# Moving the projections' evacuations behind the transposes in slots 57 to 84 of a hybrid attention trunk

## The chip, the cores and the metric

The kernel runs on one core of a Trainium2 chip. The metric is the device time in microseconds; the median of three runs of the kernel before is 633.63 us (633.28 to 633.99). PE is the matrix engine, ACT, DVE and POOL are the three elementwise engines, SP issues nearly all DMAs.

## The reference

Two layers of an encoder over 512 frames of width 1024. In each, one input projection feeds two groups of eight heads of width 64: group A is stick-breaking attention, group B softmax attention over the top 128 keys that an indexer picks, with a relative bias. Both groups are gated, concatenated and projected out; a residual and a layer norm follow.

```python
proj = jnp.einsum('bsd,dn->bsn', x, w_in)
qA, kA, vA, gA, qB, kB, vB, gB, qI, kI, wI = jnp.split(proj, SPLIT_POINTS, axis=-1)
oA = stick_breaking_attention(heads(qA, HEADS_A), heads(kA, HEADS_A), heads(vA, HEADS_A))
oB = dsa_sparse_attention(heads(qB, HEADS_B), heads(kB, HEADS_B), heads(vB, HEADS_B),
                          qI.reshape(b, s_len, IDX_HEADS, IDX_DIM), kI, wI, rel_bias, topk)
mix = jnp.concatenate([oA * jax.nn.silu(gA), oB * jax.nn.silu(gB)], axis=-1)
y = jnp.einsum('bsm,md->bsd', mix, w_out)
return layer_norm(ALPHA * x + y, ln_g, ln_b)
```

## The kernel before, in words

All matrix products are done in pairs of a high and a low half: a number is rounded to the fast format (high half, a copy on ACT), and what the rounding lost is kept as a low half (a subtraction on DVE or POOL). A projection is three matmuls for each of eight slices of the width: high by high, low by high, high by low.

The order on PE, ACT, DVE and POOL is the order in which the Python code issues (the pools run under a manual schedule). Each of these engines takes its instructions one after the other. The order on SP is made by the framework.

A layer is a loop over slots (variable `s`). Slots 0 to 23 are the indexer. From slot 24 on each slot is one block of 128 queries of one head: group A in slots 24 to 55, group B in slots 56 to 87. Head h of group B has slots 56 + 4h to 59 + 4h; its blocks `qb` 0 to 3 see 128, 256, 384 and 512 keys, so the width of an instruction tells its block. What one block of group B (class `Soft`) does is spread over several slots:

- in the slot before: POOL adds bias and mask into `p` (L821), unless that sum was stored before by DVE (L1048)
- in its slot: PE computes `z` (L573, L578); DVE adds the bias, and takes the row minimum `mn` (L830, with a second small instruction that reads `mn` out); ACT computes the exponential and its sums (L835, function `stage1b`)
- two slots later: PE transposes `p` into the PSUM tile `tr` (L585), ACT copies it out as the high half of `AT` (L593), and DVE subtracts for the low half (L596, `evacuate_lo`). For group A these are L795 and L798. There are two `tr` banks and two `z` banks
- three slots later, for the last block of a head: PE multiplies with the values (L769, `start_values` and `rest_of_values`), ACT and DVE combine the halves (L655, L657, `mix`), and POOL multiplies into `M` (L658)

Between these PE runs the projections of the units to come: `fill(...)` steps through them by a table of due times. When an accumulator is done, its evacuation is put in the list `later`, and `flush()` issues what is in the list. An evacuation of k is two ACT copies (L428, L429), two DVE subtractions (L430, L431) and two DMAs that copy halves to the other partitions (L185); of q two copies (L420, L421) and two subtractions (L422, L423); of v one of each (L413, L414); of the output projection one DVE instruction (L859). Accumulators have three PSUM banks (`pj`). The weights come by DMA; `prep_ahead` at the end of a slot splits the next one by ACT (L231) and POOL (L234).

Inside a slot the code issues: `stage0` (z), `stage2`, `stage1` (row minimum), `prepare`, `flush()`, a fill, `transpose` and `evacuate` for the older block, `stage1b` (exponential), `evacuate_lo`, the top-k, a fill, the rest.

Of the kernel before, what the change touches and what calls it, by code (L numbers as in the profile page):

```python
# [44 lines left out]
IDX_SLOTS = 24  # L45
# [24 lines left out]
SUM_SLOTS = 3  # L70
HALF_SLOTS = 5
STAGED = (46, 48)
B_PINS = (59.2, 62.5, 67, 71, 79)


# [3 lines left out]
def fills():  # L79
# [8 lines left out]
    units += [(u, both) for u in (("B", 1, "k"), ("B", 1, "q"), ("B", 1, "v"))]  # L88
    return [(u, cs, by) for (u, cs), by in zip(units, HEAD_PINS + A_PINS + B_PINS, strict=True)]

# [27 lines left out]
def tile_hybrid(ctx: ExitStack, tc: tile.TileContext, xt, x, w_in, w_ki, w_out, ln_g, ln_b, rel_bias, onehot, out, depth=DEPTH):  # L118
# [161 lines left out]
    def flush():  # L280
        while later:
            later.pop(0)()
# [330 lines left out]
    def layer(l):  # L613
# [70 lines left out]
        def split_staged(half):  # L684
            if not half:
                QKV[PAIR[1]] = vp.tile([P, NTB, 4 * P], F32R, tag="v", name="vt")
            t = slice(2 * half, 2 * half + 2)
            vv = QKV[PAIR[1]].rearrange("p t (h r) -> p t h r", r=P)[:, t]
            src = XN[:, t, W256:S].rearrange("p t (h d) -> p t h d", d=HD)
            A.activation(vv[:, :, :, :HD], src, AF.Copy)  # L690
            for i in range(2):
                G.tensor_tensor(vv[:, i, :, HD:], src[:, i], vv[:, i, :, :HD], ALU.subtract)
# [225 lines left out]
        def topk_rounds(upto):  # L918
            while rounds and 48 - len(rounds) < upto:
                qb = rounds.pop(0)  # L920
                m8 = sm.tile([P, 8], F32, tag=f"m8{qb}", name="m8", bufs=2)
                V.max(m8, scores[qb])  # L922
                V.match_replace(scores[qb], m8, scores[qb], TAKEN)  # L923
                if not rounds:
                    for b in range(1, NTB):
                        V.tensor_scalar(mask[b], scores[b], -2.0e38, MASKED, ALU.is_gt, ALU.mult)
# [40 lines left out]
        for s in range(SLOTS + 3):  # L967
# [30 lines left out]
                tasks[s].stage1()  # L998
            if isinstance(at(s + 1), Soft):
                tasks[s + 1].prepare()  # L1000
            flush()
            if not sticks[0]:
                fill(now + FRAC[0])
            for old in olds:
# [7 lines left out]
                tasks[s].stage1b()  # L1012
            for old in olds:
                old.evacuate_lo(old.head.at)
            if s >= IDX_SLOTS:
                topk_rounds(PAUSE + RATE * (s - IDX_SLOTS))
            fill(now + FRAC[1])
# [24 lines left out]
            for h in STORED:  # L1042
                if s == AHEAD[h]:
                    by_number[h].load()
                for qb, (by, tb, col) in STORED[h].items():
                    if s == by:
                        n = P * (qb + 1)
                        V.tensor_tensor(XN[:, tb, col : col + n], by_number[h].g[:, :n][:, ::-1], mask[qb], ALU.add)  # L1048
            if s in STAGED:
                split_staged(STAGED.index(s))  # L1050
            if l == 0 and s in (10, 14):
# [121 lines left out]
    for l in range(depth):  # L1173
        layer(l)
# [49 lines left out]
```

## Time and profile before

| what | value |
|---|---|
| median of 3 runs | 633.63 us |
| the profiled execution's own time | 634.15 us |
| its span | 632.3 us |
| granted clock of PE, mean | 0.998 |
| busy: PE, DVE, ACT, POOL | 620.8, 488.3, 345.2, 364.4 us |

The span runs from the first to the last instruction; 1.85 us of the execution lie around it. Busy time on PE says that matmuls were under way. Times in the timeline are microseconds from the start of the span; line numbers are those of the kernel before. Slots 57 to 84 of the first layer lie at about 196 to 270 us, those of the second layer 310.24 us later. Consecutive equal instructions stand in one row (x2, x4). A bracket at the end of a row is how long the engine stood idle before it, and what ended that.

### The profile page before, as it was taken

What the parts mean: (1) busy time and instruction counts of PE and PEld (TensorE: products, weight loads), DVE (VectorE), ACT (ScalarE), POOL (GpSimd) and SP (SyncE); (2) the same over time, 40 slices, a digit from 0 to 9 for tenths busy, and PEclk for the clock granted to TensorE, in tenths of its full rate; (3) what the DMA queues carried; (4) which work ended last, traced back from release to release, by engine and by line L of the source; (5) the groups of instructions that cost most, each with busy time, mean ns of one, the idle gap of its engine ahead of it and who ended that gap; (6) DMA issues with size and microseconds to landing.
All of it is one profiled execution on the core that took longest, in us unless ns stands there. A gap on an engine that the chain in (4) does not pass through costs nothing.

```text
span 632.3 us, 9889 instructions
## 1 busy us (share of the span) xinstructions
PE 620.8 (98%) x3309; PEld 532.3 (84%) x3309; DVE 488.3 (77%) x1050; ACT 345.2 (55%) x682; POOL 364.4 (58%) x388
## 2 busy tenths in 40 slices
PE   8999999999999999999999999999999999999995
PEld 7988888888887889888899888888888878898884
DVE  2778999899966875668845789998999567756676
ACT  4776544455357566883135855534644566678700
POOL 5553454618856676798134554525585587778721
PEclk9999999999999999999999999999999999999999
DMA  7624332141253475353313243313313444634402
GB/s 222 215 94 121 112 112 91 68 134 67 90 160 98 130 193 168 116 197 119 131 70 133 100 135 100 105 63 133 101 67 114 138 118 136 175 127 141 170 34 100
DMA packets 35688, 77.40 MB, mean 122 GB/s; under 512 B 6642, under 2 KB 15856, under 8 KB 35638
## 3 DMA queue, kind: packets, MB, share of 16 engines
q1 hardware_dynamic: 35350, 76.51, 38.2%
q8 instruction: 26, 0.43, 0.3%
q10 hardware_dynamic: 288, 0.26, 0.1%
q14 instruction: 24, 0.20, 0.1%
HBM read 61.84 MB, written 4.44 MB: 105 GB/s over the span
## 4 chain that ended last, share of the span: by engine, by line
PE 93%; DMA 2%; POOL 1%; ACT 1%; DVE 1%; SPq 1%; issue 0%; DVEq 0%; ACTq 0%; POOLq 0%
PE pj L292 15%; PE pj L294 15%; PE pj L293 15%; PE pjo L877 14%; PE o L769 6%; PE tr L585 5%; PE z L578 4%; PE z L573 4%; PE pjv L363 2%; PE pjv L361 2%; PE pjv L362 2%; PE pjv L329 2%; PE pjv L331 2%; PE pjv L330 2%; PE pjv L483 1%; DMA M<-in_w_ki_dram 1%
## 5 line engine op out<-in xcount | busy, mean ns | idle before, releaser
L234 POOL TENSOR_TENSOR wlo<-raw,whi 128x256 fp32r<-128x256 f32 (+1 forms) x254 | 228.6, 930 | 166.2 <-ACT whi L231 165.6
L292 PE MATMUL pj<-XH,whi 128*128 128x512 f32 (+1 forms) x432 | 172.1, 398 | 0.0
L294 PE MATMUL pj<-XH,wlo 128*128 128x512 f32 (+1 forms) x432 | 166.4, 385 | 0.0
L293 PE MATMUL pj<-XL,whi 128*128 128x512 f32 (+1 forms) x432 | 166.0, 384 | 0.0
L294 PEld LDWEIGHTS pj<-XH,wlo 128*128 128x128 f32 x432 | 81.1, 188 | 16.1
L292 PEld LDWEIGHTS pj<-XH,whi 128*128 128x128 f32 x432 | 81.2, 188 | 12.8
L293 PEld LDWEIGHTS pj<-XL,whi 128*128 128x128 f32 x432 | 81.4, 188 | 12.2
L785 ACT ACTIVATE om<-z 128x128 f32<-128x128 f32 (+1 forms) x64 | 28.0, 438 | 115.8 <-PE z L578 68.9
L231 ACT ACTIVATE whi<-raw 128x1024 fp32r<-128x1024 f32 x78 | 82.0, 1056 | 2.5 <-DMA raw<-in_w_in_dram 2.0
L790 DVE TENSOR_TENSOR_SCAN om<-om,future 128x128 f32<-128x128 f32 (+1 forms) x64 | 65.8, 1028 | 0.1
L922 DVE MAX8 m<-scores 128x8 f32<-128x256 f32 (+2 forms) x96 | 52.8, 550 | 0.2
L923 DVE MATCH_REPLACE8 scores<-m,scores 128x256 f32<-128x256 f32 (+2 forms) x96 | 52.1, 542 | 0.0
L658 POOL TENSOR_TENSOR M<-M,mixt 64x512 f32<-64x512 f32 x22 | 31.4, 1425 | 35.6 <-DVE mixt L657 27.7
L769 PE MATMUL o<-AT,vt 128*128 128x512 f32 (+7 forms) x256 | 48.5, 315 | 0.0
L835 ACT ACTIVATE p<-p,mn 128x128 f32<-128x128 f32 (+1 forms) x64 | 35.8, 560 | 22.0 <-DVE mn L830 21.7
L877 PE MATMUL pjo<-whi,XH 128*128 128x512 f32 (+1 forms) x118 | 41.2, 387 | 0.0
L877 PE MATMUL pjo<-wlo,XH 128*128 128x512 f32 (+1 forms) x118 | 41.0, 384 | 0.0
L578 PE MATMUL z<-k,q 128*128 128x128 f32 (+3 forms) x128 | 40.9, 320 | 0.0
L596 DVE TENSOR_TENSOR AT<-tr,AT 128x128 fp32r<-128x128 f32 (+1 forms) x64 | 31.2, 488 | 11.2 <-ACT AT L593 10.3
L877 PE MATMUL pjo<-whi,XL 128*128 128x512 f32 (+1 forms) x118 | 39.5, 381 | 0.0
L573 PE MATMUL z<-k,q 128*128 128x128 f32 (+3 forms) x128 | 39.2, 306 | 0.0
L769 PEld LDWEIGHTS o<-AT,vt 128*128 128x128 f32 (+1 forms) x256 | 32.9, 162 | 4.7 <-DVE AT L596 1.0
(172 smaller groups left out, 1271.8 us busy)
## 6 DMA issues: line engine op xcount, KB each, us to landing
raw<-in_w_in_dram SPq DMA_DIRECT2D x58, 512.0 KB
k<-k SPq DMA_DIRECT2D x32, 256.0 KB
raw<-in_w_out_dram SPq DMA_DIRECT2D x14, 512.0 KB
gbias<-f_dram SPq DMA_DIRECT2D x18, 256.0 KB
raw<-in_w_in_dram SPq DMA_DIRECT2D x16, 256.0 KB
XN<-in_x_dram SPq DMA_DIRECT2D x8, 256.0 KB
y_dram<-XN SPq DMA_DIRECT2D x4, 512.0 KB
XN<-y_dram SPq DMA_DIRECT2D x8, 256.0 KB
```

Of the source, the lines that this page charges most:

```text
L231: A.activation(hi, src, AF.Copy)
L234: low = lambda lo=lo[:, c], src=src[:, c], hi=hi[:, c]: lo_engine.tensor_tensor(lo, src, hi, ALU.subtract)
L292: T.matmul(o, w[0], XH[:, tb:, kc, :], start=first, stop=False)
L293: T.matmul(o, w[0], XL[:, tb:, kc, :], start=False, stop=False)
L294: T.matmul(o, w[1], XH[:, tb:, kc, :], start=False, stop=last)
L573: T.matmul(self.z[:, :nn], a, b, start=True, stop=False)
L578: T.matmul(self.z[:, :nn], c, d, start=False, stop=True)
L769: T.matmul(self.o[:m, sb * P :], vt[:, sb, self.hh * P : self.hh * P + m], at_block(self.at[j], sb, sb, NTB - sb), start=(sb, j) == (0, 0) ...
L790: V.tensor_tensor_scan(rev, rev, future[:, S - n :][:, ::-1], 1.0, ALU.mult, ALU.max)
L877: T.matmul(acc[:, cols], mixed[:, tb, m, :], w[:, cols], start=n == 0, stop=n == len(steps) - 1)
L922: V.max(m8, scores[qb])
L923: V.match_replace(scores[qb], m8, scores[qb], TAKEN)
```

## The change

In slots 57 to 84 of each layer, `flush()` is called behind `evacuate_lo`, in place of in front of the transposes. In the other slots nothing changes.

```diff
+FLUSH_LATE = range(IDX_SLOTS + 33, IDX_SLOTS + 61)
...
             if isinstance(at(s + 1), Soft):
                 tasks[s + 1].prepare()
-            flush()
+            if s not in FLUSH_LATE:
+                flush()
             if not sticks[0]:
                 fill(now + FRAC[0])
             for old in olds:
                 old.transpose()
                 old.evacuate(old.head.at)
...
             if isinstance(at(s), Soft):
                 tasks[s].stage1b()
             for old in olds:
                 old.evacuate_lo(old.head.at)
+            if s in FLUSH_LATE:
+                flush()
             if s >= IDX_SLOTS:
                 topk_rounds(PAUSE + RATE * (s - IDX_SLOTS))
```

The order on PE and POOL is the same in both programs. On ACT and DVE ten evacuations a layer move: k, q, k, k, q and q in slots 58, 62, 64, 66, 68 and 70; three of v in slots 72, 74 and 76; and one of the output projection in slot 84 (on DVE alone). In the rows of the changed program the line numbers are one to four higher (L836 is L835 of before, L429 is L428, L799 is L798).

ACT in slot 58 of the first layer, before; k is the projection's evacuation, AT the transposes' high half, p,sums the exponential:

```order
L835 ACTIVATE p,sums<-p,mn 128x256
L428 ACTIVATE k<-pj 64x512
L429 ACTIVATE k<-pj 64x512
L795 ACTIVATE AT_107<-tr 128x4x128
L593 ACTIVATE AT_105<-tr 128x128
L835 ACTIVATE p,sums<-p,mn 128x384
L231 ACTIVATE whi_2209<-raw_2047 128x1024
```

and now:

```order
L836 ACTIVATE p,sums<-p,mn 128x256
L796 ACTIVATE AT_107<-tr 128x4x128
L594 ACTIVATE AT_105<-tr 128x128
L836 ACTIVATE p,sums<-p,mn 128x384
L429 ACTIVATE k<-pj 64x512
L430 ACTIVATE k<-pj 64x512
L232 ACTIVATE whi_2209<-raw_2047 128x1024
```

The two copies of k moved past both high halves and past the exponential of the same slot; the weight's split stays behind them.

DVE in the same slot, before; ISA is the row minimum L830, its 128x1 row the reading of mn:

```order
L830 ISA p,mn<-z,p 128x384
L830 ISA mn 128x1
L430 TENSOR_TENSOR k<-pj,k 64x512
L431 TENSOR_TENSOR k<-pj,k 64x512
L798 SCALAR_TENSOR_TENSOR AT_108<-tr,AT_107 128x4x128
L596 TENSOR_TENSOR AT_106<-tr,AT_105 128x128
L830 ISA p,mn<-z,p 128x512
```

and now:

```order
L831 ISA p,mn<-z,p 128x384
L831 ISA mn 128x1
L799 SCALAR_TENSOR_TENSOR AT_108<-tr,AT_107 128x4x128
L597 TENSOR_TENSOR AT_106<-tr,AT_105 128x128
L431 TENSOR_TENSOR k<-pj,k 64x512
L432 TENSOR_TENSOR k<-pj,k 64x512
L831 ISA p,mn<-z,p 128x512
```

The two subtractions for k moved past both low halves, and still stand ahead of the next slot's row minimum.

ACT in slots 67 and 68, before; q is the projection's evacuation:

```order
L835 ACTIVATE p,sums<-p,mn 128x512
L420 ACTIVATE q<-pj 64x512
L421 ACTIVATE q<-pj 64x512
L593 ACTIVATE AT_105<-tr 128x3x128
L835 ACTIVATE p,sums<-p,mn 128x128
L231 ACTIVATE whi_2577<-raw_2392 128x1024
```

and now:

```order
L836 ACTIVATE p,sums<-p,mn 128x512
L594 ACTIVATE AT_105<-tr 128x3x128
L836 ACTIVATE p,sums<-p,mn 128x128
L421 ACTIVATE q<-pj 64x512
L422 ACTIVATE q<-pj 64x512
L232 ACTIVATE whi_2577<-raw_2392 128x1024
```

The q copies moved from in front of slot 68's high half to between its exponential and the weight's split.

## The prediction, as it stood before the result

> **What bounds the kernel now.** I read the page first, then windows of 10 us, then the waits, and last the timeline of the slots concerned.
>
> ```profile
> span 632.3 us, 9889 instructions
> PE 620.8 (98%) x3309; PEld 532.3 (84%) x3309; DVE 488.3 (77%) x1050; ACT 345.2 (55%) x682; POOL 364.4 (58%) x388
> ```
>
> PE sets the end: it is idle for only 632.3 - 620.8 = 11.5 us of the span. PE's own work and order are not touched by the change, so the new time is the old one, less the PE gaps that go, plus those that come. In slots 57 to 84 of the two layers the windows with a gap are these (columns: busy time of PE, PEld, DVE, ACT, POOL):
>
> ```profile
> 200.00:210.00 10.00, 9.08 (x53) 7.53 (x52) 7.48 (x17) 5.82 (x13) 8.14 (x9) 1.00 0.58 163
> 260.00:270.00 10.00, 9.99 (x55) 8.04 (x53) 6.67 (x23) 8.43 (x20) 8.36 (x6) 1.00 0.52 167
> 570.00:580.00 10.00, 9.68 (x53) 7.85 (x52) 6.15 (x23) 8.33 (x21) 7.98 (x6) 1.00 0.54 177
> ```
>
> 0.92 us is missing at 200 to 210 (slot 58), almost nothing in the rest of that layer, and 0.32 us at 574 in the second. The waits name the first gap and show who waits for whom among the helpers (us in total, times, longest):
>
> ```profile
> PE tr L585 <- DVE AT L798: 1.8, 2, 0.9
> ACT p L835 <- DVE mn L830: 21.7, 25, 2.1
> DVE k L430 <- ACT k L429: 17.5, 14, 3.9
> ```
>
> Twice, once a layer, transposes wait 0.92 us for DVE to empty a `tr` bank. The second row matters as much: ACT's exponential L835 often stands waiting for DVE's row minimum. Whatever is put behind L835 waits with it.
>
> **The change part by part.** First the gain, in slot 58 (columns: start, length, engine, line):
>
> ```profile
> 200.04 0.59 ACT L428 ACTIVATE k<-pj 64x512 fp32r<-64x512 f32 x1
> 201.23 0.56 DVE L830 CUSTOM_DVE_ANT_0 p<-z,p 128x384 f32<-128x384 f32 x1 [1.48 <-POOL p L821]
> 201.71 0.68 DVE L430 TENSOR_TENSOR k<-pj,k 64x512 fp32r<-64x512 f32 x1
> 201.92 0.62 ACT L835 ACTIVATE p<-p,mn 128x384 f32<-128x384 f32 x1
> 202.52 1.05 ACT L231 ACTIVATE whi<-raw 128x1024 fp32r<-128x1024 f32 x1
> 203.15 0.69 DVE L798 SCALAR_TENSOR_TENSOR AT<-tr,AT 128x512 fp32r<-128x512 f32 x1
> 203.89 0.44 PE L585 MATMUL tr<-ident,p 128*128 128x128 f32 x2 [0.92 <-DVE AT L798]
> 203.95 0.68 DVE L830 CUSTOM_DVE_ANT_0 p<-z,p 128x512 f32<-128x512 f32 x1
> ```
>
> L430 and L431 take 203.15 - 201.71 = 1.44 us ahead of L798. With them behind, L798 starts about 201.8, ends about 202.5, and PE, ready at 203.89 - 0.92 = 202.97, no longer waits: **-0.92 us a layer**.
>
> The price: ACT did the two k copies from 200.04, before mn was there. Now they stand behind L835, which cannot start before mn (201.8). L835 takes 202.52 - 201.92 = 0.60 until the next start, so L428 starts at 202.5 and L429 ends 1.2 us later, at 203.7. DVE's L430 needs L429, so DVE idles until 203.7, and the next row minimum L830 starts at 203.7 + 1.44 = 205.15 instead of 203.95. I call this the lag of the helpers, here 1.2 us; it costs PE nothing yet. From L830 of slot 59 the lag goes without a break through L835, mixt L655, L657 and the adds L1048 into the next row minima.
>
> The rows on which it grows, in slots 62 to 66:
>
> ```profile
> 212.53 0.56 DVE L830 CUSTOM_DVE_ANT_0 p<-z,p 128x384 f32<-128x384 f32 x1 [0.49 <-PE tr L585]
> 212.99 0.57 ACT L420 ACTIVATE q<-pj 64x512 fp32r<-64x512 f32 x1
> 214.20 0.69 DVE L422 TENSOR_TENSOR q<-pj,q 64x512 fp32r<-64x512 f32 x1 [1.10 <-ACT q L421]
> 215.16 0.60 ACT L655 ACTIVATE mixt<-o 64x512 f32<-64x512 f32 x1
> 215.85 0.67 DVE L657 TENSOR_TENSOR mixt<-o,mixt 64x512 f32<-64x512 f32 x1
> 225.06 0.69 DVE L596 TENSOR_TENSOR AT<-tr,AT 128x512 fp32r<-128x512 f32 x1
> 226.94 1.34 PE L769 MATMUL o<-AT,vt 128*128 128x512 f32 x8
> ```
>
> Slot 62: 0.5 of the lag is lost in the wait for PE before L830 (0.49), so L830 is 0.7 late (213.2) and its minimum is there at 213.75. ACT, itself 1.2 late from the weight split before, does L593 at 214.2 and L835 at 214.4, then L420 at 215.0 and L421 until 216.2 (before: 214.16). DVE does L422 and L423 from 216.2, 1.44 us, so L657 starts at 217.65: lag 1.8. Slot 64 holds it (a k copy behind an L835 of 128 columns): L596 of 225.06 moves to about 226.95 and ends at 227.6. That is PE's first real wait: the value products start at 226.94, and their second matmul needs this low half.
>
> PE's own account until here, estimated in the same way: -0.92 from slot 58, +0.35 in slot 62 (its z bank and first transpose wait for row minimum and exponential of slot 60), +0.25 in slot 65, +0.8 in slot 66, so about +0.5.
>
> ```profile
> 229.00 0.69 DVE L657 TENSOR_TENSOR mixt<-o,mixt 64x512 f32<-64x512 f32 x1 [0.30 <-ACT mixt L655]
> 234.67 0.29 DVE L830 CUSTOM_DVE_ANT_0 p<-z,p 128x128 f32<-128x128 f32 x1 [0.72 <-POOL p L821]
> 235.06 0.40 ACT L835 ACTIVATE p<-p,mn 128x128 f32<-128x128 f32 x1
> 235.46 1.04 ACT L231 ACTIVATE whi<-raw 128x1024 fp32r<-128x1024 f32 x1
> 236.58 2.54 POOL L234 TENSOR_TENSOR wlo<-raw,whi 128x512 fp32r<-128x512 f32 x2
> 240.35 0.56 DVE L830 CUSTOM_DVE_ANT_0 p<-z,p 128x384 f32<-128x384 f32 x1 [1.21 <-PE tr L585]
> 242.91 0.68 DVE L657 TENSOR_TENSOR mixt<-o,mixt 64x512 f32<-64x512 f32 x1
> 244.31 0.72 ACT L835 ACTIVATE p<-p,mn 128x512 f32<-128x512 f32 x1 [0.31 <-DVE mn L830]
> 247.04 0.60 PE L585 MATMUL tr<-ident,p 128*128 128x128 f32 x4
> ```
>
> Slot 66 adds 0.7 (L657 at 231.5, lag 2.5), which passes to POOL and to L830 of slot 68 (237.2) and L835 (237.6). There the two q copies, 1.2 us, used to run while DVE waited for POOL (0.72); now they stand between L835 and the weight split L231, which starts at 239.2: lag 3.7. POOL's wlo follows (240.3), and behind it in POOL's queue stands the bias of slot 70, so L830 of 240.35 starts at 243.75: lag 3.4. Slot 70 adds 1.3 as slot 62 did (L657 at 247.65: lag 4.7), so the exponential of 244.31 ends near 249.85. PE wants its four transposes at 247.04 + 0.5: it waits until 249.9. **PE is now 2.9 us late.**
>
> ```profile
> 246.35 1.05 ACT L231 ACTIVATE whi<-raw 128x1024 fp32r<-128x1024 f32 x1
> 252.31 0.59 ACT L655 ACTIVATE mixt<-o 64x512 f32<-64x512 f32 x1
> 262.62 0.73 ACT L835 ACTIVATE p<-p,mn 128x512 f32<-128x512 f32 x1
> 263.49 0.66 PE L585 MATMUL tr<-ident,p 128*128 128x128 f32 x4
> ```
>
> In slots 72 and 74 the v copy L413 (0.38 us) goes behind L835, in front of L231 and of L655: 252.31 becomes 257.7, lag 5.4. Slot 76 adds nothing that stays, slot 84 (one L859 behind one L596) nothing. From L655 the helpers run without slack to L835 of slot 79 and the transposes of slot 81: 262.62 + 0.73 = 263.35 ends 0.14 before 263.49. So the lag reaches PE whole: **+5.4 us in this layer**, the 0.92 already counted. The second layer repeats it 310.24 us later (its gap of 0.92 is there too). Its chain of waits comes to the same transposes with PE already waiting, so there is no slack to use up:
>
> ```profile
> 573.14 0.82 ACT p L835 x2
> ...
> 574.00 0.66 PE tr L585 x4
> ```
>
> +5.4 again.
>
> Sum: 634.15 + 10.8 = 644.95 for the profiled execution; the median lies 0.52 below it, so **644.4 us**.
>
> At nothing: PSUM banks of the projections (k of slot 58 is free at 205.2, the next unit's copy begins at 212.99, and a bank is used again by the third unit after). The Trainium skill, "PSUM — Partial Sum Buffer", "Summary: rules for kernel authors", says to evacuate promptly; by it alone PE would wait for `pj`, but these rows leave over 7 us, and the sum is the same with the rule or without. Also at nothing: the k copies between partitions and the loads behind them on SP's queue (k finished in slot 58 at 205.2 is read from slot 64 on, about 219; those of 64 and 66 in slots 72 and 80), and the weights, whose late split is still a unit ahead of its use. POOL's own order does not change.
>
> Unknown is how DVE and POOL disturb each other when shifted:
>
> ```profile
> L1048 DVE TENSOR_TENSOR XN<-gbias,mask 128x384 f32<-128x384 f32 x2 | 3.3, 1644 | 0.0
> L1048 DVE TENSOR_TENSOR XN<-gbias,mask 128x512 f32<-128x512 f32 x3 | 2.3, 772 | 0.1
> ```
>
> The narrower add takes twice the wider one, so 0.87 us rides on what runs beside it, either way, in three heads a layer: at most -2.6 to +2.6 a layer. I take 0, since shifted POOL work moves with the adds. "Perfetto Trace Analysis" of the Trainium skill, "Optimizing Scalar/DVE Operations", says that DVE and GpSimd share an SBUF port; the two rows agree with it.
>
> **The rivals.** (a) Clean gain: 0.92 goes twice, nothing comes: 634.15 - 1.84 - 0.52 = 631.8. For it: ACT is busy 55%. Against: DVE waits on the moved ACT copies at once. (b) No net change: the lag of the first heads dies in the waits for PE, and only the two v copies (0.76 a layer) reach slot 81: 2 x (0.76 - 0.92) = -0.3, so 633.3. (c) Half way: the lag dies at slot 67, where ACT had waits on transposes, and grows only from slot 68: 1.2 + 1.3 + 0.76 - 0.92 = 2.3 a layer, 638.3. Against: L1048 and L830 of slot 67 stand behind L657 on DVE itself. (d) Worse: the add's 0.87 us in three heads comes on top, 5.2 in all: 649.6.
>
> **How the numbers follow.** Forecast (own range 641 to 647) 0.58, (a) 0.07, (b) 0.07, (c) 0.2, (d) 0.08. About 0.2% is what a measurement of this kernel can tell from no change, 1.3 us. Faster is (a) alone: 0.07; within, (b): 0.07; slower 0.86. The range reaches over (c) and stops short of (a), (b) and (d): 637 to 648.
>
> **What would show it.** Right: no wait of L585 for L798 any more; DVE k L430 and q L422 waiting over 1 us in slots 58, 62, 68 and 70; PE waits at the four transposes of the heads beginning at slots 68 and 76, released by L835, of 2 us or more in all; PE busy time the same and its gaps some 11 us larger; ACT's share of the chain up. Wrong: if L830 of slot 71 is less than 3 us later against its own z product than before, the lag does not build up, and (b) or (c) holds; if L430 does not wait for L429 in slot 58, step one falls, and with it all.

## The result: slower, by less than forecast

| | before | changed |
|---|---|---|
| median of 4 runs each, us | 633.74 (633.28 to 633.99) | 641.62 (641.53 to 642.02) |
| profiled execution: its time, its span, us | 634.15, 632.3 | 641.71, 639.9 |
| granted clock of PE, mean | 0.998 | 0.997 |

The ratio is 1.0123 (95% interval 1.0111 to 1.0135). The forecast was 644.4: the sign and the place are right, the size is 2.8 us too large. In the rows below line numbers are one to four higher than before. The changed execution's records begin 0.61 us earlier: the row minimum of slot 58, which the change does not reach, starts at 200.62 here and at 201.23 before. Where I compare a start with one of before, 0.61 is added to it. Two executions among all the runs below, of 1603.56 us and of 1039.1 us (granted clock 0.557), fell into a slow state and are left out of the times.

The page of the changed kernel (span; busy time of each engine; the chain that ended last, by engine):

```profile
span 639.9 us, 9885 instructions
PE 625.1 (98%) x3309; PEld 532.3 (83%) x3309; DVE 485.3 (76%) x1050; ACT 344.2 (54%) x682; POOL 365.4 (57%) x388
PE 71%; ACT 9%; DVE 8%; POOL 5%; issue 4%; DMA 2%; SPq 0%; ACTq 0%; DVEq 0%; POOLq 0%
```

The chain was 93% PE before; now ACT, DVE and POOL hold 22% of it: PE still bounds most of the span, but from slot 57 to slot 89 (195 to 283 us, and 509 to 598 us in the second layer) the chain runs almost wholly through its helpers. Windows of 10 us (busy time of PE, PEld, DVE, ACT, POOL):

```profile
200.00:210.00 10.00, 10.00 (x56) 8.34 (x54) 6.92 (x14) 5.89 (x12) 6.93 (x7) 1.00 0.48 140
240.00:250.00 10.00, 8.58 (x67) 7.96 (x66) 5.57 (x18) 5.47 (x13) 5.00 (x6) 1.00 0.56 192
250.00:260.00 10.00, 9.29 (x72) 8.32 (x71) 4.84 (x17) 6.34 (x18) 7.62 (x7) 1.00 0.20 66
560.00:570.00 10.00, 8.32 (x60) 7.15 (x60) 4.88 (x17) 4.97 (x14) 6.83 (x7) 1.00 0.41 132
```

The gap of 0.92 at 200 to 210 is gone; the largest new gaps stand at 240 to 260, in slots 72 to 77, and in the second layer at 560 to 570. The waits behind them (us in total, times, longest):

```profile
ACT p L836 <- DVE mn L831: 48.7, 42, 3.3
DVE q L423 <- ACT q L422: 21.8, 16, 2.6
DVE k L431 <- ACT k L430: 21.0, 16, 3.9
```

The exponential's wait for the row minimum grew from 21.7 to 48.7 us, DVE's waits for the moved copies from 15.7 and 17.5 to 21.8 and 21.0. PE itself waits here, in slots 73, 77 and 81 of the first layer (timeline):

```profile
246.87 0.39 PE L574 MATMUL z<-k,q 128*128 128x256 f32 x1 [1.02 <-DVE mn L831]
247.78 0.66 PE L586 MATMUL tr<-ident,p 128*128 128x128 f32 x4 [0.40 <-ACT p L836]
258.41 0.66 PE L586 MATMUL tr<-ident,p 128*128 128x128 f32 x4 [0.41 <-ACT p L836]
266.56 0.66 PE L586 MATMUL tr<-ident,p 128*128 128x128 f32 x4 [0.26 <-ACT p L836]
```

The lag of the helpers, step by step (start in the changed kernel + 0.61, less the start before; the forecast's value beside it):

| first layer | before | changed + 0.61 | lag | forecast |
|---|---|---|---|---|
| row minimum, 512 wide, slot 59 | 203.95 | 205.15 | 1.20 | 1.2 |
| row minimum, 384 wide, slot 62 | 212.53 | 213.18 | 0.65 | 0.7 |
| mixt on DVE, slot 62 | 215.85 | 217.62 | 1.77 | 1.8 |
| row minimum, 512 wide, slot 63 | 218.87 | 219.30 | **0.43** | **1.8** |
| mixt on DVE, slot 66 | 229.00 | 229.92 | 0.92 | 2.5 |
| weight split, slot 68 | 235.46 | 237.60 | 2.14 | 3.7 |
| row minimum, 384 wide, slot 70 | 240.35 | 242.21 | 1.86 | 3.4 |
| mixt on DVE, slot 70 | 242.91 | 246.12 | 3.21 | 4.7 |
| PE, four transposes, slot 73 | 247.04 | 248.39 | 1.35 | 2.9 |
| PE, four transposes, slot 81 | 263.49 | 267.17 | 3.68 | 5.4 |

Up to mixt of slot 62 the forecast holds to 0.05. Then 1.3 us vanish between two neighbouring rows, and from there the lag runs 1.4 to 1.7 below the forecast, up to slot 81. In between stand the two stored adds. The changed kernel (DVE, POOL):

```profile
217.01 0.68 DVE L658 TENSOR_TENSOR mixt<-o,mixt 64x512 f32<-64x512 f32 x1
217.62 1.14 DVE L1052 TENSOR_TENSOR XN<-gbias,mask 128x512 f32<-128x512 f32 x2
217.77 2.14 POOL L659 TENSOR_TENSOR M<-M,mixt 64x512 f32<-64x512 f32 x1 [0.32 <-DVE mixt L658]
```

and the kernel before:

```profile
215.66 1.17 POOL L821 TENSOR_TENSOR p<-gbias,mask 128x512 f32<-128x512 f32 x1
216.45 2.50 DVE L1048 TENSOR_TENSOR XN<-gbias,mask 128x512 f32<-128x512 f32 x2
216.79 1.74 POOL L658 TENSOR_TENSOR M<-M,mixt 64x512 f32<-64x512 f32 x1
```

The same two adds take 1.14 in place of 2.50, 1.36 less, and POOL's multiply 2.14 in place of 1.74. The second layer shows the same (1.14 at 531.94). This is the term that the prediction took at 0.

### The profile page after: what moved, and what is told of

Same layout as the page of the kernel before. It is cut to its first block, busy times and chain, and to the rows that moved or that the text cites. A ratio compares the mean times of both kernels' runs of the same rounds, so it can differ in the third digit from the quotient of the medians.

```text
span 639.9 us, 9885 instructions
## 1 busy us (share of the span) xinstructions
PE 625.1 (98%) x3309; PEld 532.3 (83%) x3309; DVE 485.3 (76%) x1050; ACT 344.2 (54%) x682; POOL 365.4 (57%) x388
## 4 chain that ended last, share of the span: by engine, by line
PE 71%; ACT 9%; DVE 8%; POOL 5%; issue 4%; DMA 2%; SPq 0%; ACTq 0%; DVEq 0%; POOLq 0%
PE pj L293 12%; PE pj L295 12%; PE pj L294 12%; PE pjo L878 11%; PE o L770 3%; PE z L579 3%; ACT p L836 3%; PE z L574 3%; PE tr L586 3%; POOL wlo L235 3%; PE pjv L364 2%; PE pjv L362 2%; PE pjv L363 2%; PE pjv L484 2%; DVE p L831 2%
## 5 line engine op out<-in xcount | busy, mean ns | idle before, releaser
L836 ACT ACTIVATE p<-p,mn 128x128 f32<-128x128 f32 (+1 forms) x64 | 35.9, 560 | 48.9 <-DVE mn L831 48.7
L770 PE MATMUL o<-AT,vt 128*128 128x512 f32 (+7 forms) x256 | 50.0, 317 | 0.7 <-DVE AT L597 0.4
```

What stands on the lines that cost most here:

```text
L770: T.matmul(self.o[:m, sb * P :], vt[:, sb, self.hh * P : self.hh * P + m], at_block(self.at[j], sb, sb, NTB - sb), start=(sb, j) == (0, 0) ...
L836: A.activation(p, p, AF.Exp, bias=h.mn[:, b], scale=-1.0, accum_out=h.sums[:, b])
```

## The experiments

The theory after the result: (1) the price comes from the ACT copies, which now stand behind the exponential and so behind DVE's row minimum; (2) what the helpers are late at slot 63 passes whole to PE at slot 81; (3) the forecast is too high by the adds of slot 62 alone.

### Only DVE's half of the change

ACT issues the evacuations' copies where they were before; only DVE's subtractions (and the DMAs behind them) go behind the low halves, in slots 57 to 84.

```diff
+    def part(work):
+        if defer[0]:
+            deferred.append(work)
+        else:
+            work()
...
-        V.tensor_tensor(k[0:64, 1, :], p[0:64], k[0:64, 0, :], ALU.subtract)
+        part(lambda: V.tensor_tensor(k[0:64, 1, :], p[0:64], k[0:64, 0, :], ALU.subtract))
...
-            if s not in FLUSH_LATE:
-                flush()
+            defer[0] = s in FLUSH_LATE
+            flush()
+            defer[0] = False
...
-            if s in FLUSH_LATE:
-                flush()
+            while deferred:
+                deferred.pop(0)()
```

> The evacuations are split: their copies on ACT stand where they stood before the change, their work on DVE and the DMAs stand where the change puts them. So ACT's order is that of the kernel before, DVE's that of the changed kernel. Theory (the loss comes from the ACT copies behind the exponential L835, which waits for the row minimum): the 0.92 us stall in slot 58 goes in both layers, DVE waits for ACT's copies hardly more than before, a lag of 0.3 us or less per moved evacuation comes from DVE alone and stays within PE's margin: 632.4 us, 0.2% faster than before, range 631.7 to 633.5. Rival (the order on DVE, with the evacuation's subtractions behind the low halves, makes the loss): as slow as the change, about 641 us.

Measured: 632.13 us (631.44 to 633.54, 11 runs) against 633.81 for the kernel before on the same chip, ratio 0.9974 (0.9965 to 0.9983). So the order on ACT alone makes the difference between 641.6 and 632.1, and this version is faster than both kernels. The stall of slot 58 is gone, and the only PE wait over 0.2 us that is left in these slots of either layer is that at slot 81, 0.23 us in both:

```profile
262.78 0.66 PE L593 MATMUL tr<-ident,p 128*128 128x128 f32 x4 [0.23 <-ACT p L843]
```

### The flush between high halves and exponential

```diff
                 old.evacuate(old.head.at)
...
+            if s in FLUSH_LATE:
+                flush()
             if isinstance(at(s), Soft):
                 tasks[s].stage1b()
```

> The whole flush stands between the two: behind the high halves of the slot's transposes, ahead of the exponential, in slots 57 to 84. DVE keeps its order of before; ACT's copies no longer wait for the row minimum, only for the transposes. If the exponential in front of the copies made the whole loss, this is about the kernel before, 633.8. My theory says that any wait put in front of the ACT copies lags the helpers where they have no slack: in slot 58 the copies start behind the high halves, about 1 us later than before, and L798 with them, which makes the stall of 0.92 there nearly 2 instead of removing it; in slots 62, 64, 66 and 70 a further 0.2 to 0.8 each, part of which dies in waits for PE. I estimate +1.5 to +2 us a layer: 637, between 635.8 and 638.

Measured: 636.99 in the profiled execution, in the other three 637.94 to 640.2; ratio 1.0077 (1.0053 to 1.01). The profiled execution is where I expected it; the median of 638.86 lies 0.9 above the end of my range, and the granted clock, 0.997 in the profiled execution, was 0.995 and 0.992 in the others. The profiled execution shows where the loss comes from:

```profile
200.97 0.58 ACT L429 ACTIVATE k<-pj 64x512 fp32r<-64x512 f32 x1
202.20 0.68 DVE L431 TENSOR_TENSOR k<-pj,k 64x512 fp32r<-64x512 f32 x1 [0.90 <-ACT k L430]
203.64 0.69 DVE L799 SCALAR_TENSOR_TENSOR AT<-tr,AT 128x512 fp32r<-128x512 f32 x1
204.38 0.44 PE L586 MATMUL tr<-ident,p 128*128 128x128 f32 x2 [1.92 <-DVE AT L799]
```

The stall is 1.92 instead of 0.92, as expected. Of the later 0.2 to 0.8 that I had estimated, only 0.4 a layer reaches PE: four transposes of slot 81 at 264.42, released 0.41 late by the exponential. So the copies need not wait for the exponential to do harm: here the wait for the transposes in front of them delays DVE's low half.

### Slot 58 alone, in full

```diff
-FLUSH_LATE = range(IDX_SLOTS + 33, IDX_SLOTS + 61)
+FLUSH_LATE = range(IDX_SLOTS + 33, IDX_SLOTS + 35)
```

> The change in slots 57 and 58 alone. Theory (each moved evacuation adds its own 0.6 to 1.2 us to the helpers' lag, and PE waits when the sum passes its margin of about 2 us): the stall of 0.92 us goes, the lag of 1.2 us comes once, costs PE 0.2 to 0.7 us in slots 62 to 66 and dies before slot 73: 632.9 us, between 632.2 and 633.7. Rival (a lag once there stays to slot 81, where PE has no margin): 2 x (1.2 - 0.92) more than before, 634.3 us or above.

Measured: 634.48 (633.97 to 634.97, 11 runs), ratio 1.001 (1.0001 to 1.0019): the gain does not come, my expectation of 632.9 missed, and the rival was right. PE is 1.15 ahead at slot 61 and has given back more than that at slot 81, where it is 0.27 late:

```profile
210.35 0.45 PE L574 MATMUL z<-k,q 128*128 128x384 f32 x1 [0.21 <-DVE mn L831]
262.99 0.66 PE L586 MATMUL tr<-ident,p 128*128 128x128 f32 x4 [0.38 <-ACT p L836]
```

The 1.2 us of lag put in at slot 58 is still 0.96 at the row minimum of slot 67, 0.66 at that of slot 70 and 0.27 at mixt of slot 74, and stays there up to slot 81. I had assumed that it dies before slot 73; most of it has gone by then, but not all.

### The values alone, and the keys and queries alone

The same line with `IDX_SLOTS + 47, IDX_SLOTS + 61` (slots 71 to 84: three v copies and the output projection), and with `IDX_SLOTS + 33, IDX_SLOTS + 47` (slots 57 to 70: six k and q evacuations).

> The change in slots 71 to 84 alone, so that only the three v evacuations and one of the output projection move. Theory: the stall in slot 58 stays, the copies in slots 72 and 74 add 0.38 us each to the lag, and the whole of it reaches the transposes of slot 81: 0.76 us a layer, 635.3 us (634.8 to 635.9). Rival (the lag is absorbed, because only a large sum passes PE's margin): 633.7 us, as before.

> The change in slots 57 to 70 alone, so that only the six evacuations of k and q move. Theory (lags add up): what the change costs less the v copies' 0.76 us a layer, 641.6 - 1.5 = 640.1 us (639.3 to 640.9); the lag at the row minimum of slot 71 is the 3.2 us of the changed kernel, the transposes of slot 81 about 3 us late. Rival (PE's wait in slot 73 sets it alone, the later lag is hidden in it): 2 x 1.4 more than before, 636.5 us.

Measured: values alone 635.24 (635.06 to 635.8, 8 runs), ratio 1.0025 (1.0015 to 1.0035); keys and queries alone 640.1 (639.97 to 640.24), ratio 1.0101 (1.0085 to 1.0116). Their prices, 1.43 and 6.29, add up to 7.72, close to the 7.9 of the whole change. Both times are where I expected them if lags add up (635.3 and 640.1), and neither rival came. With the values alone the transposes of slot 81 are 0.57 later in each layer, not the 0.76 that I had; the rest comes behind that slot. With the values alone the stall of slot 58 is there as before, and in slot 81 PE waits 0.29:

```profile
202.99 0.44 PE L586 MATMUL tr<-ident,p 128*128 128x128 f32 x2 [0.92 <-DVE AT L799]
263.15 0.66 PE L586 MATMUL tr<-ident,p 128*128 128x128 f32 x4 [0.29 <-ACT p L836]
```

### More work on DVE at slot 63

The changed kernel, with the 512 wide stored add of slot 62 issued three times, to the same result.

```diff
-                        V.tensor_tensor(XN[:, tb, col : col + n], by_number[h].g[:, :n][:, ::-1], mask[qb], ALU.add)
+                        for _ in range(3 if qb == NTB - 1 and s == 62 else 1):
+                            V.tensor_tensor(XN[:, tb, col : col + n], by_number[h].g[:, :n][:, ::-1], mask[qb], ALU.add)
```

> The change, with the 512 wide add of the head read in slot 62 issued three times with the same result, about 1.2 to 1.4 us more on DVE at slot 63 in each layer: there the measured lag was 1.36 below the forecast, because the two adds took 1.14 in place of the 2.50 of before. If what the helpers are late at slot 63 passes whole to the transposes of slot 81, as my forecast had it, the time rises by 2.4 to 2.8, to 644.0 to 644.4, the forecast. If lag is absorbed on the way, it stays at 641.6 to 642.5.

Measured: 646.53 in three runs (up to 646.70), ratio 1.0201 (1.0184 to 1.0218), 4.9 over the changed kernel, twice what I had expected. The reason is that the four adds take 3.68, where I had expected some 2.4:

```profile
217.24 3.68 DVE L1053 TENSOR_TENSOR XN<-gbias,mask 128x512 f32<-128x512 f32 x4
217.39 1.67 POOL L659 TENSOR_TENSOR M<-M,mixt 64x512 f32<-64x512 f32 x1 [0.33 <-DVE mixt L658]
220.84 0.68 DVE L831 CUSTOM_DVE_ANT_0 p<-z,p 128x512 f32<-128x512 f32 x1
268.66 0.66 PE L586 MATMUL tr<-ident,p 128*128 128x128 f32 x4 [0.27 <-ACT p L836]
```

That is 2.54 more than the pair's 1.14. The rate of passage is what I wanted to know, and it is there: this execution's records begin 0.37 earlier than those of the changed kernel (transposes of slot 61 at 207.23 and 207.60), so the row minimum of slot 63 is 220.84 + 0.37 - 218.69 = 2.52 later and the transposes of slot 81 are 268.66 + 0.37 - 266.56 = 2.47 later. Point (2) holds for a lag on top of the change's own: what comes in at slot 63 passes to PE at one for one.

### The adds and POOL's multiply

Three kernels, each the changed one with one edit. First the stored adds ahead of `mix`, so that POOL's multiply cannot start beside them:

```diff
+            for h in STORED:
+                ...
             if done:
                 mix(done.head.pair, done.head.s, done.head.o, V if last else G)
...
-            for h in STORED:
-                ...
```

> The change, with the stored adds (L1052) issued on DVE ahead of the combining L656 and L658 in place of behind them, so that POOL's multiply L659, which needs L658, cannot run beside them. If it is that neighbour which stretches the adds, all pairs of adds take about 1.2 us in place of up to 2.3, POOL's multiply about 1.3 in place of 1.7 to 2.1, and of the price of the change only that part is left which does not rest on the neighbours; since the L658 of each head then waits for the adds, the gain of up to 1.1 in slots 59 and 67 is given back in part by a start of POOL's multiply that is 1.2 later: 640.5 to 642.6. Rival (the width or the place of the add, and not the multiply, sets its time): the pairs keep 2.3 where they had it, and the time is 643 or more, since L658 comes 2.3 later.

Measured: 642.73 (642.63 to 642.95), ratio 1.0141 (1.0124 to 1.0158), between the two expectations.

```profile
215.75 1.19 POOL L822 TENSOR_TENSOR p<-gbias,mask 128x512 f32<-128x512 f32 x1
216.47 1.48 DVE L1039 TENSOR_TENSOR XN<-gbias,mask 128x512 f32<-128x512 f32 x2
218.75 1.28 POOL L659 TENSOR_TENSOR M<-M,mixt 64x512 f32<-64x512 f32 x1 [1.81 <-DVE mixt L658]
```

Alone, the multiply takes 1.28. The adds still take 1.48 here, because they start while POOL's bias L822 runs on until 216.94; in slot 58 of the first layer they take 2.54 (at 205.51) beside the weight's low half and the next bias, and in slot 66, with POOL idle, 1.03 in place of 2.13. So the multiply is not special: POOL's bias and its low half of a weight stretch the adds too.

Second, a small copy on POOL ahead of the multiply; third, a narrow add on DVE ahead of the two wide ones:

```diff
+                if slow:
+                    engine.tensor_copy(t[hi, :32], t[hi, :32])
                 engine.tensor_tensor(M[hi, pair, :], M[hi, pair, :], t[hi], ALU.mult)
```

```diff
+                        if qb == NTB - 1 and s == 62:
+                            V.tensor_tensor(XN[:, tb, col : col + 16], by_number[h].g[:, n - 16 : n][:, ::-1], mask[qb][:, :16], ALU.add)
                         V.tensor_tensor(XN[:, tb, col : col + n], by_number[h].g[:, :n][:, ::-1], mask[qb], ALU.add)
```

> The change, with one small copy on POOL (64x32, onto itself) between L658 and POOL's multiply L659 of the head whose stored adds stand in slot 62, so that the multiply starts some 0.2 to 0.3 later beside the two adds. In the runs so far a multiply that starts 0.15 behind the adds leaves them at 1.14, and one that starts 0.34 behind them makes them 2.50. If the moment of the start decides, the adds take about 2.3 to 2.5 here in both layers, the helpers are 1.1 to 1.4 later, and the time rises by 2.2 to 2.8 to 643.8 to 644.4, the forecast. If it is not the moment of the start but something else that the change brought, the adds keep 1.14 and the time is 641.6 to 642.0.

> The change, with one narrow add on DVE (128x16, its result written again by the wide one) ahead of the same two adds, so that the wide adds start 0.05 to 0.1 later against POOL's multiply. In the runs so far a multiply that starts 0.11 behind the adds goes with 2.25 for the pair, one that starts 0.15 behind with 1.14. If the moment decides, the pair takes about 2.25 here and the time rises by 2.2 to 2.5, to 643.8 to 644.2; if not, by 0.1 to 0.2 a layer, 641.8 to 642.1.

Measured: the copy 641.74 to 642.37 in three runs, ratio 1.0128 (1.0112 to 1.0143), the changed kernel's time. Its profiled execution is the one of 1039.1 us, so I read nothing from it but lengths on DVE and POOL (the pairs of slots 58 and 66 have about their usual lengths there, 2.24 and 2.10): the copy starts 0.14 behind the adds and takes 0.60, the multiply follows at 0.82, and the pair takes 1.15. The copy was a bad probe: it stood in the multiply's place, and when the multiply came, the second add was under way.

The narrow add gives 645.17 (644.5 to 645.36), ratio 1.0176 (1.0162 to 1.019), some 3 over the changed kernel; the profiled execution takes 644.5, 2.8 over that of the changed kernel:

```profile
217.58 0.16 DVE L1053 TENSOR_TENSOR XN<-gbias,mask 128x16 f32<-128x16 f32 x1
217.74 1.27 POOL L659 TENSOR_TENSOR M<-M,mixt 64x512 f32<-64x512 f32 x1 [0.33 <-DVE XN L1053]
217.77 2.49 DVE L1054 TENSOR_TENSOR XN<-gbias,mask 128x512 f32<-128x512 f32 x2
220.19 0.68 DVE L831 CUSTOM_DVE_ANT_0 p<-z,p 128x512 f32<-128x512 f32 x1
227.14 1.16 PE L770 MATMUL o<-AT,vt 128*64 128x384 f32 x7 [0.43 <-DVE AT L597]
```

Here the multiply starts 0.03 ahead of the wide adds, takes its undisturbed 1.27, and the pair takes 2.49, in both layers. An instruction of 0.16 us costs 220.19 + 0.03 - 218.69 = 1.53 at the row minimum of slot 63 (these records begin 0.03 earlier: transposes of slot 57 at 199.98 and 200.01), and 268.02 + 0.03 - 266.56 = 1.49 at the transposes of slot 81. So the moment of the start matters, though pair and time went past what I had expected (2.25, 643.8 to 644.2): the profiled execution lies at the forecast's 644.4, the median 0.8 above it. PE's wait for the low half in slot 66, which the forecast had and the changed kernel does not show, is there too (last row). Point (3) holds in the main: the adds' 1.36, twice, is the largest part of the miss.

### Slot 58 alone, DVE's half

The kernel of the first experiment, in slots 57 and 58 only.

> ACT in the order of before, and DVE's subtractions behind the low halves in slots 57 and 58 alone. Slots 57 to 84 so handled gave 632.13, a gain of 1.68. My theory has the whole gain in slot 58, 0.92 a layer, and nothing in the other slots: 632.0, between 631.8 and 632.3. If the other slots carried part of that gain, this one is nearer to the kernel before: 632.6 or more.

Measured: 632.5 (632.23 to 633.25, 11 runs) against 633.88, ratio 0.9979 (0.997 to 0.9988): 1.38 gained, where slots 57 to 84 gave 1.68; the intervals overlap, so the extra is not shown. In the first experiment's kernel the two adds of slot 62 take 1.14, as in the changed one; here they take 2.52 and 2.50 as before, so the gain does not rest on them. Most of the gain is slot 58's, as the theory has it, but 1.84 it is not:

```profile
261.40 0.72 ACT L843 ACTIVATE p<-p,mn 128x512 f32<-128x512 f32 x1
262.27 0.66 PE L593 MATMUL tr<-ident,p 128*128 128x128 f32 x4 [0.40 <-ACT p L843]
```

These records begin 0.47 earlier than those of before (transposes of slot 57 at 199.72 and 200.19). PE is 1.13 ahead at slot 61, 1.14 at slot 73, and 263.49 - 262.27 - 0.47 = 0.75 at slot 81: the exponential that it needs there is only 262.62 - 261.40 - 0.47 = 0.75 earlier than before, and PE, 1.14 ahead, waits for it.

### The output projection's instruction

Two kernels that end the late slots earlier, at slot 83 and at slot 82 (`IDX_SLOTS + 60` and `IDX_SLOTS + 59` as the end of the range).

> The change in slots 57 to 83 alone; slot 84, where only the output projection's L859 moves on DVE, is as before. In the trace of the change the transposes are 3.7 late in slot 85 of the first layer and 4.1 late in the last ones; the chain there goes through the low half L597 and L860 behind it. If L860's place causes that, this kernel gains 0.4 a layer: 640.8. If slot 84 costs nothing, as I had it, 641.6.

> The change in slots 57 to 82, by which the output projection's L860 stands ahead of the low half L597 again (it is issued in slot 83 and not, as I had written, in slot 84, so the kernel that ended at slot 83 had the order of the change itself, and its 641.56 is a repeat of it). In the trace of the change the transposes are 3.7 late at slot 83 and 4.1 late in the last slots of the first layer, where the chain goes through L597 and L860 into L746 and the row minimum. If L860's place costs that, 0.24 to 0.4 a layer come back: 640.8 to 641.2. If not, 641.6.

The first measured 641.56 (641.4 to 642.05); as the second expectation says, its order is that of the change, since L859 is issued in slot 83, and the text ahead of the prediction placed it one slot too late. The second measured 641.14 (640.97 to 641.61), ratio 1.0114 (1.0098 to 1.0129); its interval and the change's overlap, and in the trace the transposes of slot 89 come 0.16 earlier. The move costs some tenths at most.

## Why the prediction was right and wrong

**Right: the gain.** L585's wait for L798 is gone in both layers, and the window of slot 58 in the first layer is full.

**Right: the mechanism.** The copies stand behind an exponential that waits for the row minimum; DVE waits for them; the next row minimum is late. The waits that were to show it do, in slots 58, 62, 68 and 70:

```profile
203.10 0.68 DVE L431 TENSOR_TENSOR k<-pj,k 64x512 fp32r<-64x512 f32 x1 [1.12 <-ACT k L430]
215.57 0.68 DVE L423 TENSOR_TENSOR q<-pj,q 64x512 fp32r<-64x512 f32 x1 [1.40 <-ACT q L422]
236.99 0.69 DVE L423 TENSOR_TENSOR q<-pj,q 64x512 fp32r<-64x512 f32 x1 [1.24 <-ACT q L422]
244.09 0.68 DVE L423 TENSOR_TENSOR q<-pj,q 64x512 fp32r<-64x512 f32 x1 [1.72 <-ACT q L422]
```

Keeping ACT's order and moving DVE's alone turned the loss into a gain of 1.7 us. The sign that would have shown the lag not to build up did not come: the row minimum of slot 71 starts 4.50 behind its z product now and 0.79 before, 3.7 later. The sign at the transposes came smaller than I had it: those of the heads at slots 68 and 76 wait 1.4 us in the two layers together, not 2.

**Right: the growth from step to step.** Behind slot 63 the lag changes by +0.5, +1.2, -0.3, +1.35 and +0.5 up to slot 81, where the forecast had +0.7, +1.2, -0.3, +1.3 and +0.7. The passage at one for one, which the sum took for granted, was measured with 2.52 in and 2.47 out, and 1.53 in and 1.49 out.

**Wrong in size: the term of the adds.** The step that failed is "I take 0, since shifted POOL work moves with the adds". It does not move with them: in slot 62 DVE's mixt came 1.77 later, by when POOL's bias L822 was done, so POOL's multiply no longer followed that bias but waited for mixt itself, and both adds got ahead of it (why the second one did stays open, see the end). The pair shrank by 1.36 in each layer, 2.7 us of a miss of 2.8. That the two figures are so close is partly luck: the steps of slot 66 and of the v copies were 0.2 smaller each than forecast, and what came on top behind slot 81, 0.4 a layer, made up for them. The bounds that the prediction gave for this term, -2.6 to +2.6 a layer, hold it; the pick of 0 inside them does not. The two rows of different width that it went by could have been told apart by what POOL did beside each add; that would have shown that this pair was the one that waited for the bias and for the multiply (2.50), so that a shift could shorten it by 1.36 and hardly lengthen it.

**Wrong, small: L859 at nothing** (at most some tenths, above), and slot 81 as the last place where lag is made: slot 89 stands at 283.11 + 0.61 - 279.62 = 4.1, 0.4 more than slot 81.

**Wrong in the reading: PE's busy time.** It was to stay the same with gaps 11 us larger. It rose by 4.3 (620.8 to 625.1), and the gaps by 3.3 only (11.5 to 14.8). The matmuls' rows overlap (those of 0.39 us start every 0.23), so waits shorter than that overlap leave no gap. The span is the sum to go by.

**The rivals.** (a), the clean gain, is what the change would have been had it moved DVE's work alone, and even that is capped at slot 81. (b) and (c), by which lag dies in waits for PE, fell at the size of the change: slot 58 alone keeps 0.96 of its 1.2 at slot 67, and in the changed kernel the 0.92 of slot 66 is still 0.92 at the row minimum of slot 67 (232.19 + 0.61 - 231.88). Their mechanism exists all the same, since of the 0.96 only 0.27 was left at slot 74. (c)'s 638.3 is 3.3 off, the forecast 2.8. (d) had a term of the adds with the wrong sign, 0.87 up in three heads for 1.36 down in one.

## What to carry to other kernels

In an engine that works in order, an instruction moved back takes over the waits of everything it is moved behind: look first at the releaser of each instruction it passes, and split an evacuation so that the engine that has nothing to gain keeps its place. How much of a lag comes out at the end depends on the waits that it meets: here 1.53 and 2.52 us on top of a lag came out whole, while 1.2 us alone were down to 0.27. A stall that goes gives PE only as much as the next helper allows. Before a contended pair of instructions is priced, look at what the other engine has under way at their start, in the old order and in the new one.

## What the runs showed of the hardware

A DVE add with both inputs in SBUF and an elementwise instruction of POOL beside it do not slow each other in proportion: one waits for the whole of the other. The pair of adds (512 and 384 wide) of slot 62:

| kernel | POOL when the adds start | pair on DVE | POOL's multiply |
|---|---|---|---|
| before | bias runs 0.38 more, multiply right behind | 2.50 | 1.74 |
| changed | idle; multiply starts 0.15 later | 1.14 | 2.14 |
| narrow add first | multiply starts 0.03 ahead | 2.49 | 1.27 |
| adds ahead of mix | bias runs 0.47 more, no multiply | 1.48 | 1.28 |

2.49 less 1.14 is 1.35, about the multiply's undisturbed 1.27; in the changed kernel it is the multiply that takes 0.86 longer, and ends 1.15 behind the pair's end, nearly its own length. The Trainium skill, "SBUF — State Buffer", "Who interferes with whom", says that a vector instruction with two SBUF inputs contends with a GpSimd instruction that reads SBUF, that the shared port pair is an exclusive lock, and that the order of issue decides who blocks. The four rows agree with the lock. They agree with the order only in part, and there the measurement decides: in the changed kernel the second add starts at 218.22, when the multiply had been under way since 217.77, and yet goes first. The first add by itself, before and in the changed kernel:

```profile
216.45 0.93 DVE L1048 TENSOR_TENSOR XN<-gbias,mask 128x512 f32<-128x512 f32 x1
```

```profile
217.62 0.67 DVE L1052 TENSOR_TENSOR XN<-gbias,mask 128x512 f32<-128x512 f32 x1
```

By that rule the wait of the first add for the bias (0.93 for 0.67, some 0.3) could have been taken off the sum beforehand; the second add's wait for the multiply could not.

What stays open is who gets the port at the boundary between two adds while POOL waits. With the multiply 0.15 behind the pair's start DVE kept it (1.14, in both layers of the changed kernel and of the first experiment's); with the same 0.15 and four adds in place of two POOL got it after the first (3.68). In slot 58 it starts 0.11 behind, and 0.40 in the second layer of the changed kernel, and gets it between the two (pair 2.27 and 2.26). The offset alone therefore does not decide, and no run here shows what does.
